# The sum of squares behind the two norms of the first block: products with a column of ones for VectorE's additions

## The chip, the cores and the metric

The kernel runs on one core of a Trainium2 chip. The time is the device time of one execution in microseconds. Three executions are known of the kernel before, and one more that the hardware profiler recorded.

## The reference, cut to what matters

The model is a first block (a mixer and a gated feed-forward net) and a second block of two layers, over 512 tokens of width 1024, all in float32. The change touches two norms of the first block, the one ahead of its feed-forward net and the one behind it, which is the first norm of the second block:

```python
def first_block(x, ...):
    ...
        mix = jnp.concatenate([out_a, out_b], axis=-1) @ w_out[l]
        x = x + rmsnorm(mix, g_mix_post[l])          # new residual
        h = rmsnorm(x, g_ffn_pre[l])                 # norm 1: needs mean(x*x) of each token
        f = (jax.nn.silu(h @ w_gate[l]) * (h @ w_up[l])) @ w_down[l]
        x = x + rmsnorm(f, g_ffn_post[l])            # new residual
    return x

def modulate(x, shift, scale):
    return rms_norm(x) * (1 + scale) + shift         # norm 2: the second block begins with it
```

Both norms need, for each of the 512 tokens, the sum of the squares of 1024 values of the new residual.

## The kernel before

Activations lie transposed: the width is on the 128 partitions in eight tiles (k = 0 to 7), the 512 tokens are the columns, so a residual `x` is a tile of 128x8x512. Each matrix product is made of three products with operands split into a high and a low half: L328 is high by high, L329 takes the low half of the activation and L330 the low half of the weight (the other way round, where the activation is the loaded operand). Below, such a product of 128x512 is called a large product. The weights come by DMA into `wraw`; ScalarE writes the high half `whi` (L316), GpSimd the low half `wlo` (L317).

`post_norm` stands at the end of both halves of the first block. It norms the block's output `y`, adds it to `x` tile by tile (L1081 on VectorE; L1082 on GpSimd for k below 5, on VectorE for the other three), and makes the factor of the next norm. For that `sqacc` squares each tile on ScalarE (L514 for the first, into `acc`, L517 for the others, into `sq`, of which there are two buffers) and VectorE adds six of the squares to `acc` (L520). `token_rstd` then multiplies `acc` and the last `sq` with a column of ones on TensorE (L417: the square is the loaded operand, 128x128 for each of four token tiles, and one column streams), so that the sums stand in PSUM with the tokens on the partitions; VectorE scales them (L419, L421) and takes the inverse root by a polynomial (`rsqrt`, L302 to L308), and `bcast_all` spreads the result over the partitions by products with the identity (L436).

The first call has `then=to_h`: each new tile of `x` goes on at once, scaled by a gain, as the input `h` of the feed-forward net (L996 on ScalarE, L997 on VectorE for the low half), and the token factor is only multiplied in behind the first products (`rb`, L1030). The call is followed by `hyena_sums` (L1986 to L1991), small products that VectorE copies out. The second call has no `then`; `modulate` (L1167 to L1171) waits for the factor before it makes the second block's input `h`. Between these steps `hyena_spectrum` and, behind the second call, the products of the context tokens give TensorE work.

The order of instructions on each engine is set when the program is built, by a scheduler that runs a timeline of its own estimates; so a change in one place can also change the order of work far behind it. Each engine works off its list in order.

Of the kernel before, what the change touches and what calls it, by code (L numbers as in the profile page):

```python
# [11 lines left out]
F32 = mybir.dt.float32  # L12
F32R = mybir.dt.float32r
I32 = mybir.dt.int32
AF = mybir.ActivationFunctionType
ALU = mybir.AluOpType
AX = mybir.AxisListType
PSUM = bass.MemoryType.PSUM
DRAM = bass.MemoryType.DRAM
P = 128  # L20
D = 1024
KD = 8
T = 512
# [200 lines left out]
class Prog:  # L224
# [847 lines left out]
    def post_norm(self, tt, ps, accs, acc, y, x, rp, spec, then=None):  # L1072


        V, G, S, PE = self.V, self.G, self.S, self.PE
        r = self.token_rstd(tt, ps, accs, 4, "t")
        self.hyena_spectrum(tt, ps, spec[0], [None, self.stats])
        pb = self.bank(ps, "t")
        known = self.bcast_all(pb, r, 4)
        for k in range(KD):  # L1080
            V.tensor_tensor(out=y[:, k], in0=y[:, k], in1=pb, op=ALU.mult)  # L1081
            (G if k < 5 else V).tensor_tensor(out=x[:, k], in0=x[:, k], in1=y[:, k], op=ALU.add)  # L1082
            if then is not None:
                then(k)
            out = self.sqacc(tt, acc, x[:, k], k, eng=V)
        r = self.token_rstd(rp, ps, out, 4, "t")
        self.hyena_spectrum(tt, ps, spec[1], [known, known])
        return r

# [1023 lines left out]
```

## Time and profile before

| | |
|---|---|
| three executions | 2554.90, 2567.63, 2569.49 us, median 2567.63 |
| the profiled execution | 2564.34 us |
| its span in the trace | 2562.6 us, so 1.7 us lie around it |
| TensorE products | busy 95% of the span |
| VectorE | busy 64% |
| GpSimd | busy 47% |
| ScalarE | busy 39% |
| granted TensorE clock, mean | 0.981 of full speed |

Times in the rows are counted from the start of the span. A granted clock of 1.00 is 2.4 GHz, one of 0.50 is 1.2 GHz. A busy TensorE isn't one at its peak, since products are pipelined: what a product costs in a stream is the distance of its start from the next one's.

### The profile page before, as it was taken

Reading aid. Unit: us, or ns where it says so; the run is one execution under the profiler, and the core shown is the slowest. Engines: PE = TensorE matmul, PEld = TensorE weight load, DVE = VectorE, ACT = ScalarE, POOL = GpSimd, SP = SyncE. Lnnn points to the kernel's source line nnn. Section 1 sums busy time; section 2 is a strip of 40 time slices with the busy share of each in tenths; the row PEclk is TensorE's granted clock in tenths of the full one; section 3 lists DMA queues with packets and bytes.
Section 4 is the critical chain, followed back from the end, with each engine's and each line's share of the span. In section 5 each row is a group of like instructions: output and inputs, shape, how many; then the busy total and the mean of one; then the engine's idle time right before and its main releaser. Section 6 shows DMA issues by size and latency. Waiting matters only on the chain.

```text
span 2562.6 us, 35342 instructions
## 1 busy us (share of the span) xinstructions
PE 2446.2 (95%) x13312; PEld 2038.3 (80%) x13312; DVE 1630.7 (64%) x2896; ACT 994.4 (39%) x1763; POOL 1196.2 (47%) x835
## 2 busy tenths in 40 slices
PE   8899999999999999887999999999999999999999
PEld 6678776878887777766788888888888888788887
DVE  6944648677775687588665776777577555534333
ACT  4526435322224433487634222122244563323322
POOL 3356526455556455587543332323245326343443
PEclk9999999999999899999999999999999999999999
DMA  4230023354454332301222343434242013232333
GB/s 145 73 111 18 26 80 136 122 178 148 162 175 140 125 109 77 103 17 34 95 104 75 126 139 101 140 105 143 73 136 79 34 58 138 78 98 88 106 99 94
DMA packets 105773, 262.13 MB, mean 102 GB/s; under 512 B 12017, under 2 KB 20337, under 8 KB 105220
## 3 DMA queue, kind: packets, MB, share of 16 engines
q1 hardware_dynamic: 105028, 258.84, 30.1%
q8 instruction: 105, 1.72, 0.3%
q10 hardware_dynamic: 576, 1.05, 0.1%
q14 instruction: 64, 0.52, 0.1%
HBM read 248.15 MB, written 16.93 MB: 103 GB/s over the span
## 4 chain that ended last, share of the span: by engine, by line
PE 77%; DVE 13%; ACT 3%; POOL 3%; issue 3%; DMA 2%; SPq 0%; POOLq 0%; ACTq 0%; DVEq 0%
PE ps_mm L330 15%; PE ps_mm L328 15%; PE ps_mm L329 15%; PE ps_mx L328 3%; PE ps_mx L329 3%; PE ps_mx L330 3%; PE ps_m L328 3%; PE ps_m L330 3%; PE ps_m L329 3%; PE ps_pv L1629 3%; PE ps_s L1622 2%; PE ps_t L440 2%; DVE h L1171 1%; DVE acc L520 1%; DVE rsq_a L305 1%
## 5 line engine op out<-in xcount | busy, mean ns | idle before, releaser
L317 POOL TENSOR_TENSOR wlo<-wraw,whi 128x1024 fp32r<-128x1024 f32 (+2 forms) x344 | 783.1, 2280 | 1064.5 <-ACT whi L316 1007.5
L316 ACT ACTIVATE whi<-wraw 128x1024 fp32r<-128x1024 f32 (+2 forms) x345 | 336.8, 978 | 888.5 <-PE ps_mm L329 475.3
L328 PE MATMUL ps_mm<-h,whi 128*128 128x512 f32 (+1 forms) x1496 | 540.3, 363 | 10.9 <-ACT whi L316 7.9
L330 PE MATMUL ps_mm<-h,wlo 128*128 128x512 f32 (+1 forms) x1496 | 539.9, 362 | 2.6 <-POOL wlo L317 2.6
L329 PE MATMUL ps_mm<-h,whi 128*128 128x512 f32 (+1 forms) x1496 | 539.5, 361 | 1.1 <-DVE h L1171 1.0
L328 PEld LDWEIGHTS ps_mm<-h,whi 128*128 128x128 f32 x1496 | 281.9, 189 | 55.5 <-ACT whi L316 7.9
L330 PEld LDWEIGHTS ps_mm<-h,wlo 128*128 128x128 f32 x1496 | 282.7, 189 | 49.2 <-POOL wlo L317 3.2
L329 PEld LDWEIGHTS ps_mm<-h,whi 128*128 128x128 f32 x1496 | 281.4, 188 | 46.3 <-DVE h L1171 1.5
L329 PE MATMUL ps_mm<-fa,whi 128*128 128x512 f32 (+1 forms) x528 | 186.9, 355 | 0.0
L330 PE MATMUL ps_mm<-fa,wlo 128*128 128x512 f32 (+1 forms) x528 | 185.5, 355 | 1.1 <-POOL wlo L317 1.1
L328 PE MATMUL ps_mm<-fa,whi 128*128 128x512 f32 (+1 forms) x528 | 185.1, 355 | 0.0
L1299 DVE SCALAR_TENSOR_TENSOR cb<-ps_mm,small,cb 128x511 f32<-128x511 f32 (+1 forms) x66 | 43.6, 660 | 188.7 <-ACT cb L1297 188.6
L1247 DVE SCALAR_TENSOR_TENSOR x<-ps_mm,mod,x 128x512 f32<-128x512 f32 x80 | 59.4, 748 | 133.0 <-PE ps_mm L330 126.2
L1117 DVE CUSTOM_DVE_ANT_0 ada_j<-ada_w,ada_c 128x512 f32<-128x512 f32 x128 | 138.9, 1085 | 5.8 <-DMA ada_w<-in_w_ada 5.4
L1117 DVE CUSTOM_DVE_ANT_0 ada_w<-ada_w,ada_c 128x512 f32<-128x512 f32 x128 | 124.3, 971 | 3.5
L1117 DVE CUSTOM_DVE_ANT_0 x<-x 128x512 f32<-128x512 f32 x128 | 122.8, 979 | 1.9
L330 PEld LDWEIGHTS ps_mm<-fa,wlo 128*128 128x128 f32 x528 | 99.2, 188 | 16.3 <-POOL wlo L317 1.7
L328 PEld LDWEIGHTS ps_mm<-fa,whi 128*128 128x128 f32 x528 | 99.1, 188 | 15.1 <-ACT whi L316 0.3
L329 PEld LDWEIGHTS ps_mm<-fa,whi 128*128 128x128 f32 x528 | 99.3, 188 | 14.7
L904 DVE TENSOR_REDUCE few<-ps_s 128x1 f32<-128x768 f32 (+1 forms) x96 | 74.0, 774 | 32.0 <-PE ps_s L1622 30.7
L440 PE MATMUL ps_t<-ident,E 128*128 128x128 f32 x464 | 77.3, 286 | 14.1 <-POOL E L1804 8.8
L329 PE MATMUL ps_mx<-h,whi 128*128 128x512 f32 x216 | 85.6, 396 | 3.8 <-DVE h L997 3.8
(500 smaller groups left out, 5210.7 us busy)
## 6 DMA issues: line engine op xcount, KB each, us to landing
wraw<-in_w_up SPq DMA_DIRECT2D x88, 512.0 KB
ada_w<-in_w_ada SPq DMA_DIRECT2D x128, 256.0 KB
wraw<-in_w_d SPq DMA_DIRECT2D x48, 384.0 KB
wraw<-in_w_d SPq DMA_DIRECT2D x53, 320.0 KB
x<-in_w_ada SPq DMA_DIRECT2D x64, 256.0 KB
wraw<-in_we_in SPq DMA_DIRECT2D x24, 512.0 KB
wraw<-in_w_g SPq DMA_DIRECT2D x22, 512.0 KB
wraw<-in_w_u SPq DMA_DIRECT2D x22, 512.0 KB
```

The source lines that it names most:

```text
L316: self.S.activation(hi[:, :n], raw[:, :n], AF.Copy)
L317: (eng or self.G).tensor_tensor(out=lo[:, :n], in0=raw[:, :n], in1=hi.bitcast(F32)[:, :n], op=ALU.subtract)
L328: mm(ps, lhi, rhi, start=start, stop=False)
L329: mm(ps, lhi, rlo, start=False, stop=False)
L330: mm(ps, llo, rhi, start=False, stop=stop)
L440: last = self.PE.transpose(ps[:, j * P:(j + 1) * P], src[:, j * P:(j + 1) * P], self.ident)
L904: V.tensor_reduce(out=m, in_=src, op=ALU.max, axis=AX.X, negate=True)
L1117: V.tensor_tensor_reduce(out=(junk, w)[s], in0=w, in1=c[:, s, i * T:i * T + T], scale=0.5, scalar=0.0, op0=ALU.mult, op1=ALU.add, accum_ou ...
L1247: V.scalar_tensor_tensor(out=xs[s][:, m], in0=p[:, :w], scalar=mod[:, gate * 8 + m, s:s + 1], in1=xs[s][:, m], op0=ALU.mult, op1=ALU.add)
L1299: V.scalar_tensor_tensor(out=cb[:, t0 + 1:t1], in0=pg[s][:, :w_ - 1], scalar=fw[0], in1=cb[:, t0 + 1:t1], op0=ALU.mult, op1=ALU.add)
L1622: self.PE.matmul(p[:, c0:min(n, c0 + 512)], q[i], k[i][:, c], start=i == 0, stop=i == 1)
L1629: self.PE.matmul(pv[64 * e:64 * e + 64, cols], vals(e, kt), pts[e][:, kt * P:(kt + 1) * P], start=kt == 0, stop=kt == nk - 1)
```

## The change

In `post_norm` the calls of `sqacc` and `token_rstd` for the new residual go. Each square goes to a tile `sq` on ScalarE, and four products with the column of ones follow for each k (32 in all, in place of 8), each into a column of its own of one PSUM bank `pq`. VectorE then sums the eight columns of each token tile with one reduction and scales the sum; the inverse root is unchanged. The squares' additions L520 of these two norms go, six in each.

```diff
             (G if k < 5 else V).tensor_tensor(out=x[:, k], in0=x[:, k], in1=y[:, k], op=ALU.add)
             if then is not None:
                 then(k)
-            out = self.sqacc(tt, acc, x[:, k], k, eng=V)
-        r = self.token_rstd(rp, ps, out, 4, "t")
+            sq = tt.tile([P, T], F32, name="sq")
+            S.activation(sq, x[:, k], AF.Square)
+            if k == 0:
+                pq = self.bank(ps, "t")
+            for t in range(4):
+                PE.matmul(pq[:, 4 * k + t:4 * k + t + 1], sq[:, t * P:(t + 1) * P], self.ones, start=True, stop=True)
+        v = tt.tile([P, 4], F32, name="ms")
+        V.tensor_reduce(out=v, in_=pq[:, :4 * KD].rearrange("p (k t) -> p t k", t=4), op=ALU.add, axis=AX.X)
+        r = self.rstd(rp, v, 4, D)
         self.hyena_spectrum(tt, ps, spec[1], [known, known])
         return r
```

The changed file has seven lines more ahead of `hyena_sums` and what follows, so that L1986 there is L1993, and L1989 is L1996.

The first place is TensorE's list in the feed-forward net's first products behind norm 1. Before, the two groups of products with ones (`acc`, then `sq`) stand together there:

```order
L329 MATMUL ps_m<-h,whi 128x512
L330 MATMUL ps_m<-h,wlo 128x512
L329 MATMUL ps_mx<-h,whi 128x512
L417 MATMUL ps_t<-ones,acc 128x1 x4
L417 MATMUL ps_t<-ones,sq 128x1 x4
L330 MATMUL ps_mx<-h,wlo 128x512
L328 MATMUL ps_mx<-h,whi 128x512
```

With the change, two groups stand ahead of the first product that takes the low half of `h`, and six are spread over the large products that follow; this is the middle of them:

```order
L328 MATMUL ps_mx<-h,whi 128x512
L1090 MATMUL ps_t<-ones,sq 128x1 x4
L329 MATMUL ps_mx<-h,whi 128x512
L330 MATMUL ps_mx<-h,wlo 128x512
L328 MATMUL ps_mx<-h,whi 128x512
L329 MATMUL ps_m<-h,whi 128x512
L330 MATMUL ps_m<-h,wlo 128x512
L1090 MATMUL ps_t<-ones,sq 128x1 x4
L329 MATMUL ps_mx<-h,whi 128x512
```

The eight products that stood together are 32 in seven places among the large ones.

The second place is VectorE's list at norm 2, from the addition of the residual to the inverse root. Before:

```order
L1081 TENSOR_TENSOR y<-y,ps_t 128x512 x8
L1082 TENSOR_TENSOR x<-x,y 128x512 x2
L520 TENSOR_TENSOR acc<-acc,sq 128x512
L1082 TENSOR_TENSOR x<-x,y 128x512
L520 TENSOR_TENSOR acc<-acc,sq 128x512 x5
L419 TENSOR_SCALAR ms<-ps_t 128x4
L421 SCALAR_TENSOR_TENSOR ms<-ps_t,ms 128x4
```

With the change:

```order
L1081 TENSOR_TENSOR y<-y,ps_t 128x512 x8
L1082 TENSOR_TENSOR x<-x,y 128x512 x3
L1092 TENSOR_REDUCE ms<-ps_t 128x4
L426 TENSOR_SCALAR ms<-ms 128x4
L302 TENSOR_SCALAR rsq_i<-ms 128x4
```

The six additions are gone from it, and the two scalings have become a reduction and a scaling.

The third place is TensorE's list at norm 2, at the products of the context tokens (`whi` and `wlo` by `h`). Before, the groups with ones come first and six large products stand between them and L436:

```order
L330 MATMUL ps_mx<-whi,h 128x512
L417 MATMUL ps_t<-ones,acc 128x1 x4
L417 MATMUL ps_t<-ones,sq 128x1 x4
L328 MATMUL ps_m<-whi,h 128x512
L329 MATMUL ps_m<-wlo,h 128x512
L330 MATMUL ps_m<-whi,h 128x512
```

With the change, the third and fourth group stand on either side of the first product that takes the new `wlo`, and after nine large products come the last four groups and, at once, L436:

```order
L328 MATMUL ps_m<-whi,h 128x512
L1090 MATMUL ps_t<-ones,sq 128x1 x4
L329 MATMUL ps_mx<-wlo,h 128x512
L1090 MATMUL ps_t<-ones,sq 128x1 x4
L330 MATMUL ps_mx<-whi,h 128x512
L328 MATMUL ps_mx<-whi,h 128x512
L329 MATMUL ps_mx<-wlo,h 128x512
L330 MATMUL ps_mx<-whi,h 128x512
L329 MATMUL ps_m<-wlo,h 128x512
```

The list goes on after one more large product with these rows:

```order
L328 MATMUL ps_m<-whi,h 128x512
L329 MATMUL ps_m<-wlo,h 128x512
L330 MATMUL ps_m<-whi,h 128x512
L1090 MATMUL ps_t<-ones,sq 128x1 x16
L436 MATMUL ps_t<-ident,rsq_i 128x128 x4
```

The last groups moved from ahead of large products to behind them, and nothing is left between them and L436.

Further on, the two attentions of the second block's first layer have the same instructions in another order on every engine; behind them the order is the old one again, but for single places.

## Rows read from the trace of the kernel before

**Rows 1.** Page: the span, busy time by engine, and the chain that ended last

```profile
span 2562.6 us, 35342 instructions
...
PE 2446.2 (95%) x13312; PEld 2038.3 (80%) x13312; DVE 1630.7 (64%) x2896; ACT 994.4 (39%) x1763; POOL 1196.2 (47%) x835
...
PE 77%; DVE 13%; ACT 3%; POOL 3%; issue 3%; DMA 2%; SPq 0%; POOLq 0%; ACTq 0%; DVEq 0%
```

**Rows 2.** Stretches: us, each engine's busy time (instructions), granted clock, DMA share, GB/s

```profile
441.00:450.00 9.00, 8.31 (x20) 6.04 (x19) 9.00 (x10) 3.75 (x6) 3.36 (x2) 0.51 0.57 194
...
854.00:863.00 9.00, 7.41 (x28) 6.54 (x28) 3.18 (x14) 0.69 (x2) 0.00 (x0) 0.50 0.00 1
```

**Rows 3.** Timeline behind norm 1: start, us, engine, line, what [idle before, releaser]

```profile
440.49 0.80 PE L329 MATMUL ps_mx<-h,whi 128*128 128x512 f32 x1 [3.08 <-DVE h L997]
...
441.50 0.63 PE L328 MATMUL ps_mx<-h,whi 128*128 128x512 f32 x1
...
441.93 0.63 PE L329 MATMUL ps_m<-h,whi 128*128 128x512 f32 x1
...
444.96 0.80 PE L329 MATMUL ps_mx<-h,whi 128*128 128x512 f32 x1 [0.69 <-DVE h L997]
...
449.82 0.41 PE L328 MATMUL ps_m<-h,whi 128*128 128x512 f32 x1
...
458.68 0.39 PE L330 MATMUL ps_m<-h,wlo 128*128 128x512 f32 x1
...
458.91 0.39 PE L329 MATMUL ps_mx<-h,whi 128*128 128x512 f32 x1
...
459.14 0.95 PE L417 MATMUL ps_t<-ones,acc 128*128 128x1 f32 x8
...
460.84 0.49 PE L330 MATMUL ps_mx<-h,wlo 128*128 128x512 f32 x1
...
474.58 0.68 DVE L1991 COPY fkn<-ps_t 1x512 f32<-1x512 f32 x1 [4.96 <-PE ps_t L1989]
...
526.66 0.80 PE L328 MATMUL ps_mx<-fa,whi 128*128 128x512 f32 x1 [4.28 <-ACT fa L323]
```

**Rows 4.** Timeline ahead of norm 1, TensorE: two groups with ones

```profile
423.25 1.05 PE L417 MATMUL ps_t<-ones,acc 128*128 128x1 f32 x8 [0.68 <-DVE acc L520]
...
425.18 1.00 PE L417 MATMUL ps_t<-ones,sq 128*128 128x1 f32 x8
...
426.61 0.63 PE L329 MATMUL ps_m<-hy_k,whi 128*128 128x512 f32 x1
...
427.04 0.63 PE L330 MATMUL ps_m<-hy_k,wlo 128*128 128x512 f32 x1
```

**Rows 5.** Timeline at norm 2

```profile
846.76 0.63 ACT L517 ACTIVATE sq<-x 128x512 f32<-128x512 f32 x1 [2.73 <-DVE acc L520]
...
848.96 0.51 PE L329 MATMUL ps_mx<-wlo,h 128*128 128x512 f32 x1 [1.15 <-POOL wlo L317]
...
849.38 3.86 DVE L520 TENSOR_TENSOR acc<-acc,sq 128x512 f32<-128x512 f32 x5
...
853.39 1.84 PE L417 MATMUL ps_t<-ones,acc 128*128 128x1 f32 x8 [2.98 <-DVE acc L520]
...
856.79 0.77 PE L328 MATMUL ps_m<-whi,h 128*128 128x512 f32 x1
...
856.97 0.16 DVE L421 SCALAR_TENSOR_TENSOR ms<-ps_t,ms 128x4 f32<-128x4 f32 x1 [1.54 <-PE ps_t L417]
...
858.69 0.16 DVE L306 SCALAR_TENSOR_TENSOR rsq_i<-rsq_a,rsq_i 128x4 f32<-128x4 f32 x1
...
859.50 1.91 PE L436 MATMUL ps_t<-ident,rsq_i 128*128 128x128 f32 x8
...
863.08 0.80 PE L328 MATMUL ps_mx<-whi,h 128*128 128x512 f32 x1 [1.67 <-ACT h L1170]
```

**Rows 6.** Stretch of the second block's two attentions

```profile
1094.00:1250.00 156.00, 129.76 (x1004) 110.61 (x1003) 127.01 (x331) 123.50 (x342) 120.35 (x174) 0.95 0.11 33
```

## The prediction

> **What bounds the kernel now.** I read the page first, then the chain of waits and the timeline around the two places that the change touches. TensorE is busy 95% of the span, and 77% of the chain that ended last is its work [rows 1]; VectorE's share of the chain is 13%. So an instruction added to TensorE's list counts in full wherever TensorE runs without a pause, and one taken from VectorE counts only where TensorE stands and waits for it.
>
> Two waits can be touched. Behind norm 1 TensorE stands 3.08 us until 440.49 and 0.69 us until 444.96, both times for the low half of `h` (L997), not for the squares' sum [rows 3]. The sum isn't waited for: its products begin at 459.14 with no pause ahead of them. At norm 2 the sum is the path: TensorE stands 2.98 us until 853.39 for the last of five additions that take 3.86 us in a row [rows 5], and the second block's first own product can't begin before the factor has gone through the inverse root, L436 and `modulate`, at 863.08.
>
> At both places the granted clock is at its low level, 0.51 from 441 to 450 and 0.50 from 854 to 863 [rows 2]. Large products start every 0.43 us there (441.50 and 441.93) and every 0.23 us at 2.4 GHz (458.68 and 458.91) [rows 3].
>
> **The price of one group.** A group is the four products with ones for one square. Two of them lie between the large products at 458.91 and 460.84 [rows 3]: 1.93 us less the 0.23 of the first large product is 1.70 us, so 0.85 us for a group at 2.4 GHz. At 1.2 GHz two take from 853.39 to 856.79 [rows 5], 1.70 us for a group. The change has eight groups where two stood: 6 x 0.85 = 5.1 us more TensorE work at each norm, if nothing hides it.
>
> **Norm 1.** Taken away: six additions L520, of which none stood on TensorE's path (worth nothing), and two groups in the stream, 1.7 us. Added: eight groups. The first two stand ahead of the product that waits until 440.49; the pause of 3.08 us hides their 1.7 us, and with their squares late the cover would be gone at 0.85 us each. The other six stand among large products that never wait for anything else: 6 x 0.85 = 5.1. In the stream that is +3.4 us. Part comes back: VectorE is held by the copy at 474.58, which waits for TensorE's L1989, and from there it works nearly without a pause toward the `fa` for which TensorE stands 4.28 us until 526.66 [rows 3]. In the changed order 106 large products stand ahead of that small one, not 109, so VectorE starts 3 x 0.23 = 0.7 us sooner relative to TensorE, and that pause shrinks by as much: **+2.7 us**. The earlier factor `rb` itself is worth nothing, since L436 stands in TensorE's list behind 88 large products and waits for its turn. ScalarE's squares now wait for a buffer that TensorE frees; behind them in ScalarE's list stand `whi` and the second block's conditioning, and I put this at nothing, since each square of 0.63 us [rows 5] has at least five large products to run beside.
>
> **Norm 2.** Before, TensorE is free for the product with the new `wlo` at 847.81 and waits 1.15 us [rows 5]. With the change it has three groups (2.55 us) and one large product (0.23) to do first and reaches it at 850.6: that wait is gone. Then one large product, the fourth group, nine large products (0.23 + 0.85 + 2.07 = 3.15 us) bring it to 853.7, and four groups (3.4) to 857.1. Before, the second group ends at 856.8. So 2.98 us of waiting are replaced by about as much added work. VectorE takes from 856.97 to 858.85 for its eleven small instructions [rows 5], 0.17 us each; one more and a wider reduction make some 2.2 us, so L436 can start at 859.4. It started at 859.50, since six large products at the low clock stood ahead of it. **Nothing gained or lost up to L436.** The removed additions no longer press on the path, but the products that replace them queue behind large ones.
>
> **The clock at norm 2** is the unseen term. Before, the low stretch begins at the pause that ends at 853.39. With the change TensorE has no pause before 857.1, then stands about 2.3 us with nothing between the groups and L436. If the low stretch begins some 3.7 us later and is as long, it covers 3.7 us more of large products, which run at about half speed: +1.8 us. The bounds: 0, if it ends where it ended; and rival one, if it begins already amid the groups. I take **+1.8**, as the low stretch behind norm 1, 440.49 to 449.82, also ran on well after the work had resumed [rows 3].
>
> **Elsewhere.** The builder's timeline shifts, and from about 1094 to 1250 us the two attentions of the second block are interleaved in another order; the same instructions, on a stretch where TensorE is busy 129.8 of 156 us [rows 6]. I take 0, with 5 us on either side, some fifth of the 26 us that it stands idle there.
>
> **Sum:** 2.7 + 0 + 1.8 = +4.5 us. Against the profiled execution's own time, 2564.34, that is 2568.8; the median of the runs shown, 2567.63, lies 3.3 us above it, and on it the sum is 2572.
>
> **Rival one, slower: the groups with ones bring the clock down.** For it: two groups at 423.25 and 425.18, with four large products between them and 0.68 us of waiting ahead, and behind them large products start every 0.43 us (426.61, 427.04) [rows 4]. Against it: the two groups at 459.14 leave the clock high [rows 3]. The Trainium skill's page "TensorE: Matmul & The Clock Gate", section "What's actually happening", says that "the default state is throttled, and activity releases the throttle"; rows 4 agree with that if a product of one column is next to no activity, and the change strews such products over both stretches. The price: 37 large products stand between the point where the clock rose again (449.82) and the last group of norm 1, 37 x 0.20 = 7.4, and six groups cost 0.85 more each, 5.1; at norm 2 it is 23 large products and six groups, 4.6 + 5.1. It decides where the low clock of 440.49 can't end before the last group. Then the sum is 2.7 + 12.5 + 9.7 = +25 us, 2592; at one of the two places alone about +14.
>
> The same page, section "LDWEIGHTS (loading the stationary operand)", gives a load 128 columns / 1.2 ns whatever the clock. That is an estimate of 0.85 us for the eight loads of a group, as rows 3 have it at 2.4 GHz, but rows 5 have 1.70 at 1.2 GHz. By the page rival one would cost 10.2 us less, 2582; the row decides.
>
> **Rival two, faster: the work follows the squares as they come.** For it: at norm 2 the squares wait for the additions (the one at 846.76 stood 2.73 us for a buffer [rows 5]); freed of them the last could end by 849, and the groups by 850.4, 6.4 us sooner than 856.8; and groups in the pause ahead of 440.49 could keep the clock up, the 19 large products from 440.49 to 449.82 x 0.20 = 3.8 us. Against it: in the list the last four groups stand behind the `wlo` product and nine others, and rows 4 speak against groups keeping a clock up. It gives 2.7 - 3.8 - 6.4 = -7.5 us, 2560.
>
> **Rival three: the attentions' new order outweighs both norms**, by up to 10 us with either sign: 2562 or 2582 with the sum above.
>
> **How the numbers follow.** Forecast 0.55, rival one 0.18 (half of it at one place only), rival two 0.12, rival three 0.10, something else 0.05. A difference under 1%, 25.7 us, is about what a measurement of this kernel can't tell from no change: its three runs lie 14.6 us apart. Only rival one in full comes near that. Slower by over 1%: 0.06, half of its full case and a part of the unnamed; faster by over 1%: 0.02, for an effect that I have not seen; within: 0.92. The range reaches from rival two to rival one, both on the profiled execution's own time: 2557 and 2590.
>
> **What would show it.** Right: no wait for `acc` at norm 2; the last group there ends near 857 and L436 begins near 859.4; a group takes 0.85 us at full clock; TensorE comes to `fa` about 2.7 us later, after a pause of some 3.6 us. Wrong: large products every 0.43 us from 449 to 463 (rival one); the last group of norm 2 done by 851 (rival two); TensorE's busy share of the attention stretch moved by more than 5 us (rival three); or a wait of a group for its square, which would mean that the two buffers hold ScalarE and TensorE in turn.

## The result and the profile after

| | median us | runs | ratio to before (95% interval) |
|---|---|---|---|
| before, beside the changed kernel | 2562.27 | 6 (2554.90 to 2569.49) | |
| changed | 2580.49 | 6 (2576.75 to 2583.52) | 1.0063 (1.0046 to 1.0080) |
| changed, measured again beside 23 runs of before (median 2566.39) | 2581.32 | 6 (2576.22 to 2584.57) | 1.0064 (1.0040 to 1.0089) |

Slower by 0.63%, some 16 us where +4.5 was forecast: within 1%, and within the range of 2557 to 2590, but 8.5 us above the forecast of 2572. The profiled execution took 2583.25 us, with a span of 2581.5.

The page after answers to [rows 1]: TensorE is busy 12.7 us longer, VectorE 9.1 us shorter, and the shares of the chain are nearly the same, so the page doesn't tell where 16 us went.

```profile
span 2581.5 us, 35509 instructions
...
PE 2458.9 (95%) x13408; PEld 2050.3 (79%) x13408; DVE 1621.6 (63%) x2884; ACT 995.1 (39%) x1763; POOL 1196.1 (46%) x835
...
PE 77%; DVE 13%; POOL 3%; issue 2%; ACT 2%; DMA 2%; SPq 0%; POOLq 0%; ACTq 0%; DVEq 0%
```

**Norm 1** in TensorE's timeline after, answering to [rows 3] (the same work stands 5.65 us later in this trace, as it was late already ahead of the norm):

```profile
442.90 1.84 PE L1090 MATMUL ps_t<-ones,sq 128*128 128x1 f32 x16
446.13 0.50 PE L329 MATMUL ps_mx<-h,whi 128*128 128x512 f32 x1 [1.39 <-DVE h L997]
...
450.60 0.50 PE L329 MATMUL ps_mx<-h,whi 128*128 128x512 f32 x1 [2.37 <-DVE h L997]
...
452.06 0.63 PE L328 MATMUL ps_m<-h,whi 128*128 128x512 f32 x1
452.49 0.63 PE L329 MATMUL ps_mx<-h,whi 128*128 128x512 f32 x1
...
454.20 1.35 PE L1090 MATMUL ps_t<-ones,sq 128*128 128x1 f32 x8
```

The first two groups lie in the pause, as forecast: it shrinks from 3.08 to 1.39 us, and the product behind it starts at the same moment (446.13 less 5.65 is 440.48; before 440.49). For the work behind that pause, where [rows 2] have a granted clock of 0.51, this trace has 1.00, and the low stretch comes only behind the next pause (stretches of TensorE's time, with the granted clock behind the busy time):

```profile
446.10:451.60 5.50, 3.10 (x12) 1.00 0.75 263
451.60:455.40 3.80, 3.80 (x15) 0.55 0.64 210
```

That gave nothing back, since TensorE reached the second low half of `h` sooner and stood 2.37 us for it, not 0.69. Nor is it shown to be the groups' doing. The changed kernel's second trace has the same groups in the same pause and runs the same work at 0.51; the kernel with the second norm alone (both are told of below) has no group in that pause and runs it at 1.00. Their stretches, in this order:

```profile
439.80:449.10 9.30, 8.60 (x22) 0.51 0.70 234
```

```profile
444.00:449.40 5.40, 3.07 (x12) 1.00 0.78 252
```

The pause ahead of `fa` is 4.28 us as before, not 3.6:

```profile
535.45 0.80 PE L328 MATMUL ps_mx<-fa,whi 128*128 128x512 f32 x1 [4.28 <-ACT fa L323]
```

**Norm 2**, TensorE and VectorE, answering to [rows 5]; the same work stands 8.43 us later here at 844 us:

```profile
853.33 1.84 PE L1090 MATMUL ps_t<-ones,sq 128*128 128x1 f32 x16
855.03 0.48 PE L329 MATMUL ps_mx<-wlo,h 128*128 128x512 f32 x1
...
858.11 0.95 PE L1090 MATMUL ps_t<-ones,sq 128*128 128x1 f32 x8
858.91 0.48 PE L329 MATMUL ps_mx<-wlo,h 128*128 128x512 f32 x1
...
862.20 4.66 PE L1090 MATMUL ps_t<-ones,sq 128*128 128x1 f32 x32
869.16 2.04 PE L436 MATMUL ps_t<-ident,rsq_i 128*128 128x128 f32 x8 [2.31 <-DVE rsq_i L306]
872.88 0.79 PE L328 MATMUL ps_mx<-whi,h 128*128 128x512 f32 x1 [1.67 <-ACT h L1177]
...
866.89 0.19 DVE L1092 TENSOR_REDUCE ms<-ps_t 128x4 f32<-128x32 f32 x1 [12.03 <-PE ps_t L1090]
```

The waits of 1.15 and 2.98 us are gone, and no product waits for `acc`. Two groups take 1.70 us (853.33 to 855.03). But the last four take 4.66 us and not 3.4, because the clock falls under them, with no pause of TensorE ahead; these are stretches of TensorE's time, with the granted clock behind the busy time of PEld, DVE, ACT and POOL:

```profile
862.00:864.00 2.00, 2.00 (x19) 1.96 (x17) 0.00 (x0) 0.63 (x1) 0.00 (x0) 1.00 0.00 0
864.00:870.00 6.00, 3.69 (x21) 3.64 (x21) 1.82 (x12) 0.63 (x1) 0.00 (x0) 0.55 0.01 3
```

**The two attentions**, the stretch that answers to [rows 6]: TensorE is busy 122.6 of 156 us where it was 129.8.

```profile
1107.90:1263.90 156.00, 122.60 (x936) 106.59 (x935) 125.09 (x321) 118.67 (x328) 115.71 (x166) 0.91 0.11 33
```

**Where the two traces part.** I took the start of the same large product in both timelines, and the difference at several points. Two stretches are surprises: 9.4 us between 329 and 436 us, ahead of everything that the change touches, and 6.6 us in the attentions.

| stretch of the trace before, us | changed | changed, second trace | before, second trace |
|---|---|---|---|
| start to 329 | -3.8 | -0.7 | -0.4 |
| 329 to 436 (code untouched) | +9.4 | 0.0 | 0.0 |
| norm 1: 436 to 475 | +3.2 | +3.6 | -0.1 |
| 475 to 844 | -0.4 | -0.6 | -0.2 |
| norm 2: 844 to 877 | +2.4 | +2.4 | -2.3 |
| 877 to 1092 | +2.9 | +1.7 | +2.4 |
| attentions: 1092 to 1250 | +6.6 | +7.7 | +3.2 |
| rest | -1.2 | -2.2 | -0.5 |
| whole | +19.1 | +12.0 | +2.1 |

The changed kernel's first trace is 3.8 us ahead at 329 us, so of the 9.4 us it is 5.7 us late at 436 us; the second trace is 0.7 us early there.

### The profile page after: what moved, and what is told of

The parts are those of the page before. It is cut to its first block, busy times and chain, and to the rows that moved or that the text cites. A ratio compares the mean times of both kernels' runs of the same rounds, so it can differ in the third digit from the quotient of the medians.

```text
span 2581.5 us, 35509 instructions
## 1 busy us (share of the span) xinstructions
PE 2458.9 (95%) x13408; PEld 2050.3 (79%) x13408; DVE 1621.6 (63%) x2884; ACT 995.1 (39%) x1763; POOL 1196.1 (46%) x835
## 4 chain that ended last, share of the span: by engine, by line
PE 77%; DVE 13%; POOL 3%; issue 2%; ACT 2%; DMA 2%; SPq 0%; POOLq 0%; ACTq 0%; DVEq 0%
PE ps_mm L328 15%; PE ps_mm L330 15%; PE ps_mm L329 15%; PE ps_mx L328 3%; PE ps_mx L329 3%; PE ps_mx L330 3%; PE ps_m L328 3%; PE ps_m L330 3%; PE ps_m L329 3%; PE ps_pv L1636 2%; PE ps_t L440 2%; PE ps_s L1629 2%; DVE h L1178 1%; DVE rsq_a L305 1%; PE ps_t L436 1%
```

## The experiments

The table shows for each kernel the same differences of its trace against the first trace of before, and its timed ratio. "Old" and "new" is the attentions' order of instructions, as before or as in the changed kernel.

| kernel | order | 329 to 436 | norm 1 | norm 2 | attentions | ratio (95% interval) |
|---|---|---|---|---|---|---|
| changed | new | +9.4 | +3.2 | +2.4 | +6.6 | 1.0063 (1.0046 to 1.0080) |
| first norm alone | old | 0.0 | +3.7 | -2.3 | +2.9 | 1.0026 (1.0009 to 1.0043) |
| second norm alone | old, but a few rows | +5.5 | -0.5 | +1.5 | +2.9 | 1.0011 (0.9993 to 1.0029) |
| light groups at both | old | +5.5 | +0.4 | -1.3 | +2.9 | 1.0018 (1.0001 to 1.0035) |
| squares in `y` | new, but some rows | +9.4 | +7.8 | +1.9 | +8.0 | 1.0060 (1.0041 to 1.0079) |
| light first | old | -1.6 | +1.0 | +2.4 | 0.0 | 1.0021 (1.0008 to 1.0034) |
| light second | new | +9.4 | +3.1 | -2.0 | +6.4 | 1.0048 (1.0032 to 1.0064) |
| row second | old, but a few rows | +5.5 | -0.6 | -1.5 | +3.3 | 1.0021 (1.0008 to 1.0035) |
| changed, old order | old | +5.5 | +3.1 | +2.6 | +0.4 | 1.0044 (1.0028 to 1.0061) |
| row, squares in `h` | old | 0.0 | -0.1 | -3.2 | +3.2 | 1.0005 (0.9988 to 1.0022) |

For the two kernels with light groups at norm 1 the difference is taken at 477 us, since the two small products of L1989 stand some large products later in their lists. A stretch that isn't in the table, 475 to 844 us, lies -3.5 to +2.3 us from the first trace of before in these ten.

**Theory and rivals.** After the two traces my theory (A) was that the loss is a sum of places: some 3 us at norm 1, some 4 at norm 2 with the clock behind it, some 5 or more from the attentions' new order, and the 9.4 us ahead of norm 1 by chance of the clock. Rival B: the order is worth nothing, the norms carry all. Rival C: the loss ahead of norm 1 belongs to the change.

**One norm at a time**, the products with ones behind a condition, VectorE's additions in the other call:

```diff
+            if spec[0] == 0:      # in the second kernel: == 2
                 sq = tt.tile([P, T], F32, name="sq")
                 ...
+            else:
+                out = self.sqacc(tt, acc, x[:, k], k, eng=V)
```

> Only the first norm has the products with ones; the second keeps VectorE's additions, and the attentions keep the order of before. Theory A (the traces of before and after: +3.2 us at norm 1, +2.4 at norm 2 and +2.0 in the low-clock stretch behind it, +6.6 in the attentions' new order, and +9.4 between 329 and 437 us, in code that the change doesn't touch, by chance of the clock): +3 us against before, TensorE's lead over before of 3.2 us from 437 to 475 us, nothing more at norm 2 (below 0.5) or in the attentions (below 1); the stretch from 329 to 437 us may cost 9 us more or not, whatever the kernel. Rival B (the attentions' order is worth nothing and the two norms carry all of the +16): +8 us. Rival C (the loss ahead of norm 1 belongs to the change): +12, with the low clock near 350 to 375 us in it.

> Only the second norm has the products with ones; the first keeps the additions, and the attentions' order differs from before at a few rows only. Theory A: +4.4 us against before (+2.4 up to the first products of modulate, +2.0 by the clock behind it), and in the attentions below 2 us. Rival B: +8 us. Rival C: as A, since nothing ahead of norm 1 is changed; a low clock near 350 to 375 us here, where all is as before up to 814 us, would speak against C.

Measured +0.26% and +0.11%, 6.7 and 2.8 us, each uncertain by some 4.5. In the trace norm 1 costs 3.7 us; the attentions keep their order in the first kernel row for row. A's figures for the other places were missed: it had below 1 us in the attentions and below 0.5 at norm 2 for the first kernel, and the trace has +2.9 and -2.3 with unchanged lists there. The two timed differences together are 9.5 us, less than the change's 16. That would fit something that comes with both and that neither has alone, such as the new order, but with their errors the sum doesn't show it; the pairs below do. B's +8 is outside the second kernel's interval and within the first's. Against C: the kernel with the second norm alone has the code of before up to 814 us, and lost 5.5 us between 329 and 436 too. This is TensorE's stretch from 345 to 380 us there:

```profile
345.00:380.00 35.00, 32.89 (x149) 0.76 0.29 85
```

**Light groups.** Squares and ones in fp32r; a group is 4 rows of TensorE's list instead of 8.

```diff
-            sq = tt.tile([P, T], F32, name="sq")
+            sq = tt.tile([P, T], F32R, name="sq")
...
-                PE.matmul(pq[:, 4 * k + t:4 * k + t + 1], sq[:, t * P:(t + 1) * P], self.ones, start=True, stop=True)
+                PE.matmul(pq[:, 8 * k + 2 * t:8 * k + 2 * t + 2], sq[:, t * P:(t + 1) * P], onr, start=True, stop=True)
```

> Both norms as in the change, but the squares are written in fp32r and multiplied with two columns of ones in fp32r (the squares are rounded to that type), so that a group is 4 rows of TensorE's list and not 8; the attentions stand in the order of before. Theory A: a group takes 0.43 us and not 0.85; of the 2 x 6 x 0.85 = 10.2 us of added products half goes (5.1), the attentions' 6.6 go: after less 11 us, about +1 to +3 against before. If the attentions' order is worth nothing (B): after less 5, about +11. If a group doesn't become shorter: after less 6.6 by A, less 0 by B.

Measured +0.18%, 4.6 us, a little above A's +1 to +3 and far from B's +11. In its trace norm 1 costs 0.4 us, not over 3; norm 2 is 1.3 us shorter than in the first trace of before, and the attentions stand where the old order has them.

**Squares in `y`.** The square goes over the piece of `y` that is used up, so that ScalarE needs no buffer from TensorE.

```diff
-            sq = tt.tile([P, T], F32, name="sq")
+            sq = y[:, k]
```

> Both norms as in the change, but each square is written over the piece of y that is used up and not into one of two buffers, so that ScalarE doesn't wait for TensorE's groups; the groups stand earlier in TensorE's list, and the attentions stand in a third order. Theory A: ScalarE's waits for ps_t at L1086 (6.06, 2.59, 1.44 at norm 1, 3.25 and 2.33 at norm 2) are gone; at norm 2 the last group ends some 4 to 8 us sooner against the first products there, L436 as much, and the time is after less 5, with the attentions' third order at plus or minus 6. Rival D (the two buffers cost nothing, since TensorE works anyway and the same products stand behind): after within 2 us apart from the attentions. Rival E (TensorE waits for the squares with large products queued behind the groups): norm 2 is longer than after's, by 3 us or more.

The 5 us that theory A promised didn't come: 1.0060, as the changed kernel. In the time rival D holds; in the trace the parts differ: at norm 2 it is 0.5 us better than the changed kernel, and at norm 1 it is 4.6 us worse. That isn't E's way, since TensorE doesn't wait for the squares. ScalarE's waits are gone, the groups come earlier and stand close together, and the clock falls under them. TensorE's timeline at norm 2, and then stretches of it (the granted clock stands behind the busy time and count):

```profile
858.02 1.70 PE L1090 MATMUL ps_t<-ones,y 128*128 128x1 f32 x8
...
860.58 6.82 PE L1090 MATMUL ps_t<-ones,y 128*128 128x1 f32 x32
867.26 0.77 PE L330 MATMUL ps_mx<-whi,h 128*128 128x512 f32 x1
```

```profile
854.00:858.00 4.00, 4.00 (x30) 0.96 1.02 381
858.00:862.00 4.00, 4.00 (x19) 0.50 0.57 207
```

TensorE is busy without a pause from 846 us to L436 at 873.59, and still the clock halves; four groups then take 860.58 to 867.26, 1.67 us each. That is the mechanism of the prediction's rival one, which I had given 0.18.

**Light first, light second.** Two kernels that have one light norm and one of the change's each, with the light form of the third kernel behind a condition:

```diff
+            if spec[0] == 0:      # in the sixth kernel the two forms change places
+                sq = tt.tile([P, T], F32R, name="sq")
                 ...
+            else:
                 sq = tt.tile([P, T], F32, name="sq")
                 ...
```

> Light groups (fp32r, 4 rows; the squares are rounded to that type) at the first norm, the change's groups at the second; the attentions stand in the order of before, row for row. It has as many full and light groups as the next kernel, which has the change's new order there. Theory A (the new order costs 4 to 6.5 us): about +7 us against before, 5 us less than the next kernel, and in the trace no more than 3 us lost between 1100 and 1250 us. Rival B (the order is worth nothing): the same as the next kernel within 2 us.

> The change's groups at the first norm, light groups at the second; the attentions stand in the change's new order but for two rows. Theory A: about +12 us against before, 6 us or so lost between 1100 and 1250 us. Rival B: about +8, as the kernel ahead, and no more than 3 us lost there.

Measured +0.21% and +0.48%: 7 us apart, with as many full and light groups in both. Their intervals overlap by a hair (1.0034 and 1.0032), the traces don't: 0.0 and +6.4 us in the attentions. By the traces B falls. By the times alone it would not: the kernel with the new order has the 9.4 us ahead of norm 1 in its trace as well, and whether its timed runs have them isn't known.

**The row.** At the second norm the ones are the weights, and the sums of eight products of 512 columns add up in PSUM.

```diff
+                PE.matmul(pq[0:1], onr, sq, start=k == 0, stop=k == KD - 1)
...
+            row = tt.tile([1, T], F32, name="ssrow", bufs=1)
+            S.activation(row, pq[0:1], AF.Copy)
+            pt = self.bank(ps, "t")
+            for t in range(4):
+                PE.matmul(pt[:, t:t + 1], row[0:1, t * P:(t + 1) * P], self.ones[0:1], start=True, stop=True)
```

> The first norm as before. At the second the ones are the weights: eight products of one row of 512 in fp32r (the squares are rounded to that type) that add up in PSUM, then a copy of the row and four small products that turn it; the attentions stand in the order of before but for a few rows. If a product of 512 columns counts for the clock as the large ones do (theory F), the eight products cost 8 x 0.23 = 1.8 us, the clock stays high until the copy, and the time is before less 2 to 5 us: of before's 2.98 us of waiting and of its 10 us at the low clock a part goes, and the copy (0.6 us) and the turning (0.85 us) come on the path. Rival G (one column of weights is next to no activity, as one column of data is): as the second norm alone of the change, +1 to +4 us.

At norm 2 it is 1.5 us shorter than the first trace of before and 0.8 longer than the second (2.3 shorter); the whole is slower by 0.21% and not faster. F's gain doesn't show; G's reason for that isn't borne out by the next kernel. Where the 5 us of the whole come from stays open: this one trace has +5.5 ahead of norm 1 and +2.8 behind 1250 us, in code that it shares with before.

**The products alone.** The kernel before, with products of no use among the large ones of the feed-forward net, where TensorE never waits:

```diff
+                        if nm == "w1_g" and m in (3, 6, 9, 13, 16):
+                            u = self.bank(ps, "t")
+                            for i in range({3: 16, 6: 32, 9: 32, 13: 64, 16: 16}[m]):
+                                if m < 9:
+                                    PE.matmul(u[:, i:i + 1], self.ident, self.ones, start=True, stop=True)
+                                elif m < 16:
+                                    PE.matmul(u[:, 2 * i:2 * i + 2], w[0][:, :P], act[0][0][:, :2], start=True, stop=True)
+                                else:
+                                    PE.matmul(u[0:1], w[0][:, :1], act[0][0], start=True, stop=True)
```

> Before, with products of no use among the large products of the feed-forward net, where TensorE never waits and its clock is high: 4 groups with ones in a row (m=3), 8 in a row (m=6), 8 light ones (m=9), 16 light ones (m=13), 16 products of one row of 512 (m=16), and 8 groups with three large products ahead of each (m=19). Rival one of the prediction, as the fourth kernel's trace now bears it out (TensorE without a pause, and the clock low from 858 us amid groups): behind 8 groups in a row (6.8 us) and 16 light ones (6.8 us) the granted clock falls to 0.5 and the large products start every 0.43 us for some us; behind 4 groups or 8 light ones (3.4 us) it may; strewn groups leave it high or not as the share of their time decides (0.85 of 1.54 us). Rival H (only pauses bring the clock down, what happened at 858 us was chance): 1.00 behind all of them. The 16 rows of 512 take 0.23 us each and leave the clock high (F) or not (G). A group takes 0.85 us at the high clock, a light one 0.43. The whole: +31 us and what the low clock costs, 2 to 4 us at each place where it comes.

The stretches of TensorE ahead of, in and behind the first run (four groups), and then in and behind eight light groups, sixteen rows of 512, and six of the strewn groups:

```profile
488.00:491.30 3.30, 3.30 (x16) 1.00 0.15 14
491.30:495.40 4.10, 4.10 (x33) 0.85 0.81 254
495.40:501.10 5.70, 5.70 (x15) 0.51 0.47 160
...
609.60:613.20 3.60, 3.60 (x34) 1.00 0.76 250
613.20:617.20 4.00, 4.00 (x12) 0.57 0.01 4
...
735.60:739.50 3.90, 3.90 (x18) 1.00 0.44 137
739.50:743.00 3.50, 3.50 (x18) 1.00 0.01 4
...
797.60:806.60 9.00, 9.00 (x66) 1.00 0.60 216
806.60:811.00 4.40, 4.40 (x20) 1.00 0.77 268
```

TensorE is busy all the time. Four groups in a row bring the clock to 0.51 for the 5.7 us behind them: 13 large products that take 0.43 us and not 0.23, 2.6 us lost. Eight groups and sixteen light ones do the same (0.50 for 4.9 and 5.4 us behind them). Groups with three large products between them leave it at 1.00, and so do sixteen products of one row of 512, at 0.23 us each: F, not G. H falls. A light group takes 0.44 us (609.65 to 613.14 for eight). Counted by how much later the large products behind each place start, less the place's own products, the four places where the clock fell lost 3.4, 4.8, 1.7 and 5.0 us, the rows and the six strewn groups nothing. This one execution was 42 us above before's median and its stretch from 475 to 844 us 38.9 us longer: 31 us of products and 14.9 us of low clock, of which some 6 us came back at and behind the pause ahead of `fa` (0.9 us, where it was 4.28).

The Trainium skill's page "TensorE: Matmul & The Clock Gate", section "What's actually happening", has the throttled clock as the default and activity as what releases it. This trace agrees with it in part only: TensorE was busy without a pause both where the clock fell (four groups, 4.10 of 4.10 us, 0.85 and then 0.51) and where it stayed at 1.00 (rows of 512, 3.90 of 3.90 us), so the busy time doesn't tell the two cases apart.

**The changed kernel with the old order.** Three idle stores behind the factor of the second norm move the builder's timeline; nothing else is changed.

```diff
+        if spec[0] == 2:
+            nu = tt.tile([P, T], F32, name="sq")
+            for _ in range(3):
+                V.memset(nu, 0.0)
         self.hyena_spectrum(tt, ps, spec[1], [known, known])
```

> The changed kernel with three idle stores of 128x512 on VectorE behind the second norm's factor; they move the builder's timeline, and the attentions stand again in the order of before, row for row. Both norms are the change's. Theory A (the new order of the attentions costs 5 to 7 us): after less 5 to 7, about +9 to +10 against before. Rival B (the order is worth nothing, the difference of the fifth and sixth kernel came from elsewhere): as after, +15. The stores themselves, three on VectorE while it waits for the spread factor, cost nothing or up to 1 us.

+0.44%, 11.3 us, beside +0.64% for the changed kernel in the same session: 5.1 us by the ratios, 4.8 by the medians. The intervals overlap; with the pair above and the traces the order is worth 5 to 7 us. What TensorE waits for in that stretch, in the changed kernel, in this one and in the first trace of before (total us, times, longest); L1811, L1815 and L1804 are the same line:

```profile
PE ps_t L440 <- POOL E L1811: 17.7, 12, 4.0
PE ps_t L440 <- DVE da_o L1832: 5.9, 1, 5.9
```

```profile
PE ps_t L440 <- POOL E L1815: 9.4, 7, 4.0
...
PE ps_t L440 <- DVE da_o L1836: 3.6, 1, 3.6
```

```profile
PE ps_t L440 <- POOL E L1804: 8.8, 8, 2.8
PE ps_t L440 <- DVE da_o L1825: 4.7, 1, 4.7
```

In the new order TensorE comes twelve times to a transposition of `E` before GpSimd has added its two parts, not seven times; that is 8.3 us more of waiting. All four traces with the new order have eleven or twelve such waits, some 17 us. TensorE's busy time there is 130.31 of 156 us with the old order, as before:

```profile
1104.70:1260.70 156.00, 130.31 (x1000) 110.53 (x999) 125.94 (x331) 123.67 (x341) 120.75 (x173) 0.93 0.12 33
```

**The row with squares in `h`**, a try at a version that beats both, with one idle store that keeps the old order:

```diff
-                sq = tt.tile([P, T], F32R, name="sq")
+                sq = old[:, 0, k]     # h, the feed-forward net's input, used up
```

> The first norm as before. At the second the eight products of one row of 512 of the seventh kernel, but the squares go into the high half of the net's input h, which is used up and is of type fp32r, so that no square waits for a buffer; one idle store on VectorE keeps the attentions in the order of before. The squares can follow x as it comes: if the second norm of before loses its time to the additions and to the pauses, L436 begins 5 to 8 us sooner against the first products there, and the time is before less 3 to 6. If the large products that stand ahead of L436 and the low clock set it anyway, 0 to 2 us sooner, and the time is that of before within 3.

L436 begins 4.8 us sooner against the products at 844 us, the norm is 3.2 us shorter by 877 us than in the first trace of before and 0.9 than in the second; the whole is the time of before (1.0005). TensorE now runs out of large products ahead of the factor, stands 1.98 us for it and 1.73 us for `modulate`, and the low clock follows the pauses (timeline, then stretches):

```profile
854.35 2.08 PE L436 MATMUL ps_t<-ident,rsq_i 128*128 128x128 f32 x8 [1.98 <-DVE rsq_i L306]
858.16 0.79 PE L328 MATMUL ps_mx<-whi,h 128*128 128x512 f32 x1 [1.73 <-ACT h L1191]
```

```profile
850.00:854.00 4.00, 2.36 (x15) 1.00 0.26 100
854.00:862.00 8.00, 5.92 (x17) 0.50 0.00 1
```

**Both kernels once more**, unchanged:

> The changed kernel as it is, beside the others on the same chip: +13 to +18 us against before. Its trace shows once more what the clock does between 329 and 437 us, ahead of all that the change touches: by chance anything from 1.00 to 0.61 from 345 to 380 us; 0.61 again would be the third of the changed kernel's like, and leave open that the stretch goes with the kernel.

> The kernel before as it is, for a second trace: the stretches that no kernel changes (345 to 380, 475 to 814 and 877 to 1100 us) may lie 0 to 9, 0 to 4 and 0 to 3 us from the first trace's, by the clock alone.

The changed kernel's ratio is the same (1.0064). TensorE's stretch from 345 to 380 us, in its first trace and then in its second:

```profile
345.00:380.00 35.00, 33.09 (x130) 0.61 0.22 60
```

```profile
345.00:380.00 35.00, 32.87 (x179) 1.00 0.37 117
```

At 1.00 there the second trace loses nothing between 329 and 436 us. So the 9.4 us ahead of norm 1 don't come with the change each time, and C falls as it was stated; that they come more often with it isn't excluded, as the last section says. Before's second trace differs from its first by -2.3 us at norm 2 and +3.2 in the attentions, with the same instructions in the same order. At norm 2 that is the clock's: from 859 to 866 us it is 0.50 in the first trace and 1.00 in the second. In the attentions, from 1094 to 1215 us, it is 0.93 and 0.89, with some 25 us of waiting in both.

## Why the prediction held, and where it was off

- **The sum.** Forecast +4.5, measured +16 (12 to 20 by the interval). It was met within its range because that is 33 us wide; the sum itself was too small by a factor of more than three. The traces account for some 12: norm 1 with the change +3.1 to +3.7 (five traces; -0.6 to 0 in the unchanged ones), norm 2 +1.5 to +2.6 (five traces; -2.3 to 0 in four of unchanged code, so some 3.8 between the means), the attentions' order some 5. The other 4 are within the interval and aren't explained; a share of the loss between 329 and 436 us would fit and isn't shown.
- **Elsewhere, the step that failed.** "I take 0, with 5 us on either side": 6.4 to 8.0 in four traces with the new order, 0.0 to 3.4 in ten with the old one or nearly so; the means lie 5 us apart. It was rival three, with a chance of 0.10 and 2582 as its slower case, and its sign in the profile came as stated: TensorE's busy time there moved by 7.2 us. The same instructions in another order aren't free where an engine's list is worked off in order and TensorE waits for three other engines.
- **Norm 1.** Forecast +2.7, in the traces +3.2 and +3.6. The 3.4 us in the stream were right: two groups hidden in the pause, six added at 0.85 or so (the first of them took 1.21 us, partly at 1.2 GHz). The 0.7 us that should come back at `fa` did not. VectorE does start 0.68 us sooner relative to TensorE (its copy at 482.69, 8.11 us later than before, where TensorE is 8.79 late), but then waits 2.96 us instead of 2.29 for `fth`: ahead of L1032 in ScalarE's list stands a `whi` that waits for TensorE.
- **Norm 2 up to L436.** Forecast 0, measured +1.2: the last group ends at 858.4 and L436 begins at 860.7 by the clock of before (less 8.43), for 857 and 859.4. The groups' count and order were right; the four at the end ran partly at 1.2 GHz, 1.26 us more than 3.4.
- **The clock at norm 2.** Forecast +1.8, measured +1.2 between L436 and 877 us, so 2.4 in all where 1.8 was the sum. The low stretch does end 3.5 us later than in the first trace of before, about as forecast. The reason was wrong: I let it begin at TensorE's pause behind the groups, and it began under them, as rival one says. It struck at the end of norm 2 alone; elsewhere at most two groups stand together. And the trace that the sum was worked out from was a slow one here: three others with the same norm 2 are 1.3 to 2.3 us shorter.
- **Rival two's parts.** The clock did stay high behind the first pause in one trace, and it was worth nothing, because the next wait took the time. That groups in the pause keep it up isn't borne out: with the same groups the second trace has 0.51 there, and without any the kernel with the second norm alone has 1.00. [rows 4], which I held against it, don't decide either: behind the same two groups (430.51 and 432.44 in the changed kernel's first trace) the clock is 1.00 from 427 to 436 us.
- **Squares' buffers at nothing:** no product waits for a square at either norm, as forecast. The kernel without ScalarE's waits is no faster, but its groups also stand closer together, so it doesn't price the buffers alone.
- **The price of a load.** The Trainium skill's page "TensorE: Matmul & The Clock Gate", section "LDWEIGHTS (loading the stationary operand)", gives one formula by the number of columns and names no clock level; at 0.50 the eight loads of a group took 1.67 us, at 1.00 0.85. The rows decide, as the prediction had it.

## What to carry to other kernels

Where a scheduler places the work, compare the two lists of instructions as a whole: a change of a few microseconds in one place can put another stage in a worse order, and that was the largest single term here; a harmless nudge that restores the old order prices it. Products of one column in a row can cost more than their own time: four groups alone took 3.4 us and lost as much again, since the clock fell under them. With large products between them, or turned so that the ones are the weights, it stayed up here, though neither form made this kernel faster than before. And take a second trace of the same kernel before pricing a place below 3 us.

## What the hardware showed unexpectedly

- TensorE's clock falls to 1.2 GHz without any pause: 5.7 us at 0.51 behind four groups in a row (4.1 us with what the falling clock cost them); it stayed at 1.00 with six strewn groups and with sixteen rows of 512.
- The same instructions ran at 1.00, 0.76 or 0.61 in the same 35 us (345 to 380 us) in different executions, worth about 0, 5.5 and 9.4 us between 329 and 436. Three of the four traces with the new order have 0.61 and none of the ten with the old one; the fourth has 1.00. The lists of TensorE are the same up to there in all of them. What decides it, and how often the timed runs have it, stays open.
